# Drawing up the engines' order with the timeline simulator in a hybrid attention and long-convolution block

## The chip, the cores and the metric

The kernel runs on one core of one Trainium2 chip. Five engines with an instruction queue each do the work: TensorE (matmuls; "PE" in the profile, its weight loads "PEld"), VectorE ("DVE"), ScalarE ("ACT"), GpSimd ("POOL") and SyncE ("SP"), which here only issues DMAs. Each engine takes its own instructions strictly in the order in which the program lists them; between engines, semaphores tell when an input is there or a buffer is free. The metric is the time of one execution in microseconds, as the median of three runs.

## The reference

One trunk layer of a diffusion backbone over 1024 latent tokens of width 1024, with 256 context tokens beside them, all in float32:

```python
h = modulate(rmsnorm(x, norm1_g[i]), sh1, sc1)
q, k, v, hv, hx1, hx2, gna, ghy = jnp.split(h @ w_in[i], IN_SPLITS, axis=-1)
y_na = neighbourhood_attention(to_heads(q), to_heads(k), to_heads(v),
                               to_heads(k_c), to_heads(v_c), na_rpb[i])
y_hy = hyena_mixer(hv, hx1, hx2, *hy_params)
x = x + g1 * gated_merge(gna, ghy, y_na, y_hy, w_na_o[i], w_hy_o[i], w_out[i])
h2 = modulate(rmsnorm(x, norm2_g[i]), sh2, sc2)
x = x + g2 * swiglu(h2, ffn_w1[i], ffn_w3[i], ffn_w2[i])
...
return rmsnorm(x, final_g)
```

The shifts, scales and gates (sh1, sc1, g1 and so on) are rows of silu(c) @ w_ada + b_ada. The attention has 8 heads of width 64; each query sees a window of 8 x 16 of the 16 x 64 grid, with a learned bias, and all context keys. The Hyena mixer is a short convolution followed by two gated long convolutions over all 1024 tokens, with filters that a small network makes, computed by Fourier transforms. The feed-forward part has a hidden width of 2816.

## The kernel before

**Arithmetic.** Most products run on operands that are split into a high and a low part of a faster float32 form: `split` (L175 casts on ScalarE, L176 subtracts on VectorE), and `gemm` or `product` then does three matmuls for each 128-deep step, low by high, high by low, high by high. Transposes and Fourier matrices use plain float32. The feed-forward products use a scheme with seven block products in place of eight (operands named h2_1 to h2_7).

**Stages.** `hidden` loads x, makes the first norm's transposed activations and the first adaptive-norm rows from eight 1 MB pieces of w_ada (tiles `wada`, L297, three buffers; products at L299 into `ada_ps`). `project` makes the 40 column blocks of the input projection, each in two halves of 512 tokens, 24 matmuls a half (L195, `in_ps`). Beside it, `side` runs the Hyena filters (`filters`: `filt_ps` L363, times the decay factors `dec` on VectorE at L370), the remaining adaptive-norm rows (`ada_rows`, VectorE at L890 on tiles `wal`), and then four long convolutions (`conv`, transforms `dft_ps` L442 to L444, with matrices `matf` and `mati`). Each convolution goes through seven steps, in which the forward transform of a class, the product with the filter's spectrum, the inverse transform and the combination on VectorE are a step apart from each other. Then `attention` takes 32 items (a pair of heads, a row block, a column block): scores (`s_ps`, L766 and L769), softmax (VectorE L774, ScalarE L775), transposes (`pt_ps` L786), copy (`pts`, L790), values (L800), copy to `yrow` (L807); the last projection halves and the Hyena output (`hy_ps`) run between the items. `mix` and `rows` merge both branches (`na_ps`, `out_ps` L1109), then `ffn_early`, `ffn_up` (`x_ps`, `y_ps`, `z_ps`, L1171) and `ffn_down` (`dx_ps`, `dy_ps`, `dz_ps`, L1340) follow, with `close` and `finish` for the output.

**What sets the order.** The kernel's Python code traces all instructions in one program order; generators are merged by weights (`_merged`, with `SIDE` = 496 for the side work against 39 for the projection, and yields that tell the weight of a step). The order on each engine is not that one. When the TileContext closes, a scheduler draws it up: it steps a simulated machine through time, and whenever an engine of that machine can take another instruction, it gives it the ready one of the lowest priority number, which is the place in the program order. Ready means that, on the simulated machine, what it depends on is done and a buffer of its pool is free. So the durations that the simulated machine assigns decide which of two instructions gets ahead of the other, on the five engines and among the DMAs of each queue, and which buffer of a ring a tile gets. On the chip the lists are then fixed: nothing is picked again.

Two devices bend this. `tc.high_priority()` gives what is traced in it an earlier priority (projection weights, the short convolution's taps, some loads of the feed-forward part). `tc.keep_in_program_order(x)` ties an instruction behind the one traced before it on its engine, whatever the simulated machine says. So pinned are the filters' matmuls but the first of each four, the score, transpose and value matmuls of attention, the projection's matmuls after `self.pinned` is set (the part that runs between attention items), the Hyena output's matmuls, the first matmul of each early feed-forward product, and loads of w2 in `ffn_down`. The matmuls of the projection before that, the transforms, the merge and the rest of the feed-forward part are free.

The library has two simulated machines. The plain one, used before, gives each instruction a duration and an engine; the timeline simulator turns each into a list of events on devices (an engine's sequencer, its queue of issued instructions, the engine itself, the DMA hardware) and steps these. The first is also the one whose optimism about landed inputs the library's text on `keep_in_program_order` speaks of.

Of the kernel before, what the change touches and what calls it, by code (L numbers as in the profile page):

```python
# [1455 lines left out]
def program(nc, shapes):  # L1456
    args = {n: nc.dram_tensor(f"in_{n}", s, F32, kind="ExternalInput").ap() for n, s in shapes.items()}
    out = nc.dram_tensor("out_y", (T, D), F32, kind="ExternalOutput").ap()
    with tile.TileContext(nc) as tc:
        Block(tc, args, out).run()  # L1460


# [9 lines left out]
```

## Time and profile before

| | |
|---|---|
| median of 3 runs (lowest, highest) | 1711.23 us (1708.59, 1711.89) |
| profiled execution, span from first to last instruction | 1711.4 us |
| that span against the median | 0.2 us above it |
| TensorE busy | 1657.6 us, 97% |
| its weight loads | 1307.2 us, 76% |
| VectorE, ScalarE, GpSimd busy | 1230.1, 662.6, 153.3 us |
| mean granted TensorE clock | 0.993 |
| moved by DMA | 282.48 MB, 165 GB/s |

The profile shows one execution. A line of a timeline gives start, busy time, engine, source line, operation and tiles; a bracket at its end tells how long the engine was idle before it and what ended that. "PEclk" is the granted share of TensorE's full clock. Lines of waits give the waiting engine and tile, what it waited for, the total, how often, and the longest.

### The profile page before, as it was taken

The page shows a single profiled execution, that of the slowest core. Times are in us where ns is not written, and L with a number is a line of the kernel's source. Part 1 is how long each engine was busy: PE and PEld are TensorE (multiplying, and loading weights), DVE is VectorE, ACT ScalarE, POOL GpSimd, SP SyncE. Part 2 cuts the span into 40 slices and gives each one's busy share as a digit, 9 for nine tenths or more (in the row PEclk, how much of TensorE's full clock was granted, in tenths as well). Part 3 has the DMA queues.
Part 4 walks back from the last instruction along what each step waited for, and adds up shares of the span by engine and source line. Part 5 has one row for each costly group of instructions (what it writes and reads, how often), then busy time and mean ns, then how long its engine had stood idle before and what let it go on. Part 6 is the DMA issues. An engine that isn't in the chain of part 4 may idle for free.

```text
span 1711.4 us, 22611 instructions
## 1 busy us (share of the span) xinstructions
PE 1657.6 (97%) x8124; PEld 1307.2 (76%) x8124; DVE 1230.1 (72%) x2076; ACT 662.6 (39%) x1141; POOL 153.3 (9%) x274
## 2 busy tenths in 40 slices
PE   6898999999999999999999999999999999999997
PEld 2676776777777778888787888888888888878886
DVE  3697586699995966465865967867865566479576
ACT  4621221312221224455654315733333333355455
POOL 0100211101010014020200000010101011000000
PEclk9999999999999999999999999999999999999999
DMA  9276854645553456344657524333423223395334
GB/s 364 103 255 199 266 173 158 215 139 187 167 201 137 160 187 186 126 148 131 197 174 245 187 65 160 124 124 117 160 99 110 94 99 109 105 383 177 98 120 154
DMA packets 114517, 282.48 MB, mean 165 GB/s; under 512 B 15840, under 2 KB 24676, under 8 KB 112102
## 3 DMA queue, kind: packets, MB, share of 16 engines
q1 hardware_dynamic: 94472, 219.99, 38.6%
q0 software_dynamic: 19280, 60.60, 10.5%
q8 instruction: 64, 1.05, 0.3%
q10 hardware_dynamic: 653, 0.44, 0.1%
q14 instruction: 48, 0.39, 0.1%
HBM read 213.60 MB, written 67.39 MB: 164 GB/s over the span
## 4 chain that ended last, share of the span: by engine, by line
PE 65%; issue 10%; DVE 4%; DMA 2%; ACT 1%; POOL 1%; SPq 0%; DVEq 0%; POOLq 0%; ACTq 0%
PE x_ps L1171 15%; PE in_ps L195 12%; PE z_ps L1171 7%; PE dx_ps L1340 6%; PE out_ps L1109 4%; PE dz_ps L1340 3%; PE hy_ps L195 2%; PE y_ps L1171 2%; PE dft_ps L442 2%; PE pt_ps L800 2%; PE pt_ps L786 2%; PE na_ps L195 2%; PE dy_ps L1340 1%; PE s_ps L766 1%; PE dft_ps L444 1%
## 5 line engine op out<-in xcount | busy, mean ns | idle before, releaser
L195 PE MATMUL in_ps<-hTh,wl 128*128 128x512 f32 x640 | 260.0, 407 | 0.9 <-ACT proj L614 0.5
L195 PE MATMUL in_ps<-hTl,wh 128*128 128x512 f32 x640 | 254.5, 398 | 0.4 <-DVE hTl L176 0.2
L195 PE MATMUL in_ps<-hTh,wh 128*128 128x512 f32 x640 | 253.9, 397 | 0.0
L195 PEld LDWEIGHTS in_ps<-hTh,wl 128*128 128x128 f32 x640 | 121.5, 190 | 32.2 <-issue 5.6
L195 PEld LDWEIGHTS in_ps<-hTl,wh 128*128 128x128 f32 x640 | 121.8, 190 | 27.1 <-DVE hTl L176 1.8
L195 PEld LDWEIGHTS in_ps<-hTh,wh 128*128 128x128 f32 x640 | 121.6, 190 | 26.9 <-issue 0.4
L175 ACT CAST wh<-wr 128x1024 fp32r<-128x1024 f32 (+1 forms) x56 | 51.9, 926 | 141.4 <-PE in_ps L195 110.0
L176 DVE TENSOR_TENSOR wl<-wr,wh 128x1024 fp32r<-128x1024 f32 (+1 forms) x56 | 59.8, 1067 | 63.2 <-ACT wh L175 63.1
L176 DVE TENSOR_TENSOR ol<-ws,oh 128x512 fp32r<-128x512 f32 x88 | 60.4, 688 | 50.6 <-ACT oh L175 50.3
L176 DVE TENSOR_TENSOR ol<-ar,oh 128x512 fp32r<-128x512 f32 x77 | 52.8, 687 | 47.7 <-ACT oh L175 47.7
L175 ACT CAST oh<-ar 128x512 fp32r<-128x512 f32 x77 | 47.9, 622 | 84.4 <-PE dx_ps L1340 33.1
L175 ACT CAST oh<-ws 128x512 fp32r<-128x512 f32 x88 | 54.7, 622 | 57.1 <-PE x_ps L1171 27.5
L442 PE MATMUL dft_ps<-a,matf 128*128 128x512 f32 x128 | 67.1, 606 | 5.0 <-DVE a L430 4.1
L775 ACT ACTIVATE pe<-pe,mx 128x640 f32<-128x640 f32 x64 | 52.6, 822 | 48.9 <-DVE mx L774 48.9
L1340 PE MATMUL dx_ps<-ol,oh 128*128 128x512 f32 x176 | 68.7, 390 | 1.7 <-DVE ol L176 1.7
L774 DVE CUSTOM_DVE_ANT_0 pe<-s_ps,bias 128x640 f32<-128x640 f32 x64 | 50.1, 820 | 28.1 <-PE s_ps L769 28.1
L1340 PE MATMUL dx_ps<-oh,ol 128*128 128x512 f32 x176 | 67.4, 390 | 1.9 <-DVE ol L176 1.9
L1340 PE MATMUL dx_ps<-oh 128*128 128x512 f32 x176 | 68.5, 389 | 0.0
L176 DVE TENSOR_TENSOR ol<-wr,oh 128x512 fp32r<-128x512 f32 x70 | 48.0, 688 | 22.3 <-ACT oh L175 22.2
L175 ACT CAST oh<-wr 128x512 fp32r<-128x512 f32 x70 | 43.3, 622 | 52.3 <-PE x_ps L1171 16.0
L890 DVE SCALAR_TENSOR_TENSOR aacc<-wal,cs,aacc 128x512 f32<-128x512 f32 x56 | 41.8, 747 | 23.1 <-DMA wal<-in_w_ada 22.5
L1111 DVE TENSOR_TENSOR x<-x,out_ps 128x512 f32<-128x512 f32 x64 | 42.6, 683 | 15.2 <-PE out_ps L1109 15.0
(394 smaller groups left out, 4193.7 us busy)
## 6 DMA issues: line engine op xcount, KB each, us to landing
wr<-in_w SPq DMA_DIRECT2D x52, 512.0 KB, 3.4
wr<-in_w_in SPq DMA_DIRECT2D x40, 512.0 KB, 4.2
ar<-g SPq DMA_DIRECT2D x77, 256.0 KB, 2.8
wal<-in_w_ada SPq DMA_DIRECT2D x64, 256.0 KB, 4.1
matf<-in_dft_f SPq DMA_DIRECT2D x32, 384.0 KB, 4.7
bias<-in_rpb SPq DMA_DIRECT2D x64, 192.0 KB, 3.7
g<-t POOLq DMA_DIRECT2D x47, 256.0 KB, 3.0
w<-in_w SPq DMA_DIRECT2D x44, 256.0 KB, 5.4
```

The costliest lines, as they stand in the source:

```text
L175: self.nc.scalar.copy(hi, src)
L176: self.nc.vector.tensor_sub(lo, src, hi.bitcast(F32))
L195: mm = nc.tensor.matmul(ps, ww[:, k * P:(k + 1) * P], xx[:, k, pos:pos + width], start=(i == 0), stop=(i == n - 1))
L442: nc.tensor.matmul(ps, m[:, 0], v.rearrange("p a b -> p (a b)"), start=True, stop=False)
L774: nc.vector.tensor_tensor_reduce(pe, ps[:, 256:896], bt, -1.0, 3e38, ALU.add, ALU.min, mx[:, 0:1])
L775: nc.scalar.activation(pe, pe, AF.Exp, bias=mx[:, 0:1], scale=-1.0, accum_out=mx[:, 1:2])
L786: pin(nc.tensor.transpose(pt[:, at:at + P], pe[:, c * P:(c + 1) * P], self.ident))
L890: nc.vector.scalar_tensor_tensor(acc, w, c, acc, op0=ALU.mult, op1=ALU.add)
L1109: nc.tensor.matmul(ps, gg[x][:, tk], ww[y][:, sl], start=(i == 0), stop=(i == n - 1))
L1111: nc.vector.tensor_add(x1[:, sl], x1[:, sl], ps)
L1171: mm = nc.tensor.matmul(ps, w[u][:, k * P:(k + 1) * P], x[v][:, k, :], start=(start and k == 0 and i == 0), stop=(stop and k == 3 and i == 2),
L1340: nc.tensor.matmul(ps[j], x[u][:, j * P:(j + 1) * P], w[v], start=(start and i == 0 and c == 0), stop=(stop and i == N - 1 and k == len(re ...
```

## The change

The scheduler steps the timeline simulator in place of the plain machine. No instruction is added, removed or altered, no tile, pool, pin or weight. What may come out otherwise is the order on each engine and DMA queue, the buffer that a tile gets, and with these the semaphore waits.

```diff
@@ -1456,7 +1456,7 @@
 def program(nc, shapes):
     args = {n: nc.dram_tensor(f"in_{n}", s, F32, kind="ExternalInput").ap() for n, s in shapes.items()}
     out = nc.dram_tensor("out_y", (T, D), F32, kind="ExternalOutput").ap()
-    with tile.TileContext(nc) as tc:
+    with tile.TileContext(nc, schedule_with_timeline_sim=True) as tc:
         Block(tc, args, out).run()
```

## The prediction

> **What bounds the kernel now.** I read the page first: which engine is busy, and for how much of the span.
>
> ```profile
> span 1711.4 us, 22611 instructions
> PE 1657.6 (97%) x8124; PEld 1307.2 (76%) x8124; DVE 1230.1 (72%) x2076; ACT 662.6 (39%) x1141; POOL 153.3 (9%) x274
> GB/s 364 103 255 199 266 173 158 215 139 187 167 201 137 160 187 186 126 148 131 197 174 245 187 65 160 124 124 117 160 99 110 94 99 109 105 383 177 98 120 154
> ```
>
> TensorE works 97% of the span; it is without work for 1711.4 - 1657.6 = 53.8 us. The profiled span lies 0.2 us above the median of the three runs, 1711.23 us, so a sum made against it holds for the median too. The change leaves every instruction as it is and alters only in which order each engine takes its own. It can then gain at most where TensorE waits, and it can lose wherever TensorE is now kept fed. So the second view is the busy time by stage: start (to 75 us), filters beside the input projection (to 350), long convolutions beside it (to 560), the way over to attention (to 680), attention (to 925), merge (to 1070), the up half of the feed-forward part (to 1490) and its down half.
>
> ```profile
> core 0: us, PE busy (x) PEld busy (x) DVE busy (x) ACT busy (x) POOL busy (x), PEclk, DMA share, GB/s
> 0.00:75.00 75.00, 57.54 (x276) 33.19 (x276) 41.73 (x72) 46.06 (x75) 2.48 (x9) 1.00 0.59 230
> 75.00:350.00 275.00, 258.52 (x1188) 193.29 (x1187) 201.75 (x292) 61.62 (x98) 36.02 (x61) 0.96 0.64 209
> 350.00:560.00 210.00, 210.00 (x887) 159.91 (x885) 183.43 (x317) 48.79 (x69) 15.84 (x23) 1.00 0.52 172
> 560.00:680.00 120.00, 118.13 (x524) 92.19 (x524) 93.43 (x166) 34.91 (x55) 24.78 (x45) 1.00 0.55 180
> 680.00:925.00 245.00, 240.50 (x1848) 194.50 (x1847) 153.11 (x352) 132.52 (x248) 28.38 (x51) 1.00 0.51 157
> 925.00:1070.00 145.00, 143.85 (x646) 117.89 (x644) 111.86 (x164) 55.48 (x88) 4.26 (x8) 1.00 0.47 158
> 1070.00:1490.00 420.00, 419.06 (x1848) 344.36 (x1848) 282.39 (x442) 170.99 (x294) 39.18 (x73) 1.00 0.33 112
> 1490.00:1711.40 221.40, 210.01 (x920) 171.83 (x918) 162.44 (x276) 112.17 (x214) 2.40 (x5) 0.99 0.56 188
> sum 1711.40, PE 1657.63 PEld 1307.17 DVE 1230.14 ACT 662.56 POOL 153.34; mean PE 207.20 PEld 163.40 DVE 153.77 ACT 82.82 POOL 19.17
> ```
>
> Taking busy from length, the idle time is 17.5, 16.5, 0, 1.9, 4.5, 1.2, 0.9 and 11.4 us. The reader is to see how lopsided this is: from 350 to 1490 us, two thirds of the kernel, only 8.5 us can be won, and every microsecond of a new misfit is lost. The filter stage, with 16.5 us, is the one place where another order has something to find. There the clock column also stands at 0.96.
>
> [...]
>
> **The filter stage, where a gain can be.** TensorE takes its instructions in the drawn order, so one matmul drawn too early holds up all behind it. Two such places, from the timelines:
>
> ```profile
> 83.45 0.39 PE L195 MATMUL in_ps<-hTh,wh 128*128 128x512 f32 x1
> 86.26 1.13 PE L363 MATMUL filt_ps<-fw,hid 64*128 64x256 f32 x6 [2.42 <-DVE fv L370]
> ...
> 87.90 0.63 PE L195 MATMUL in_ps<-hTl,wh 128*128 128x512 f32 x1
> ...
> 90.46 0.54 PE L195 MATMUL in_ps<-hTl,wh 128*128 128x512 f32 x1
> ```
>
> ```profile
> 137.25 0.39 PE L195 MATMUL in_ps<-hTh,wh 128*128 128x512 f32 x1
> 137.25 0.19 PEld L195 LDWEIGHTS in_ps<-hTh,wl 128*128 128x128 f32 x1
> 137.48 0.39 PE L195 MATMUL in_ps<-hTh,wl 128*128 128x512 f32 x1
> 141.46 1.39 DVE L370 TENSOR_TENSOR fv<-filt_ps,dec 128x512 f32<-128x512 f32 x2 [3.67 <-DMA dec<-in_decay]
> ...
> 142.21 2.07 PE L363 MATMUL filt_ps<-fw,hid 64*128 64x256 f32 x6 [4.33 <-DVE fv L370]
> ...
> 144.80 0.63 PE L195 MATMUL in_ps<-hTh,wh 128*128 128x512 f32 x1
> ...
> 148.64 0.47 PE L195 MATMUL in_ps<-hTh,wh 128*128 128x512 f32 x1
> ```
>
> At 137.48 a half of the projection (24 matmuls for 512 tokens) has begun, is cut by six filter matmuls, and goes on at 144 us: its other matmuls had all they need. The filter matmuls wait for a PSUM bank that VectorE frees, and VectorE waits 3.67 us for the decay factors' DMA. The plain model had those landed sooner. A model that follows the transfers more closely would draw the filter matmuls later, behind ready ones. Each stall has a second price: after it the projection's matmuls start 0.43 us apart (nine of them in 148.64 - 144.80 = 3.84 us) instead of 0.23 (137.25 to 137.48): 3.84 - 9 x 0.228 = 1.79 us. After the first stall six take 90.46 - 87.90 = 2.56 us, 1.19 us too much. So the two are worth 4.33 + 1.79 and 2.42 + 1.19: **-9.7 us**, which I take in full. Bounds: 0, if the new order misses as often elsewhere, and all 16.5 us of the stage with 1.79 + 1.19 on top.
>
> [...]
>
> **The start.** The adaptive-norm rows need eight 1 MB loads, and the order on SP's queue decides what goes before them.
>
> ```profile
> L299 PE MATMUL ada_ps<-wada,cs 128*32 128x512 f32 x64 | 13.7, 959 | 6.3 <-DMA wada<-in_w_ada 6.3
> ```
>
> A simulator in which the first product ends later frees the three wada buffers later, and puts other ready loads ahead on the queue. One 512 KB load at the first slice's 364 GB/s takes 0.524 / 0.364 = 1.4 us. I take one such load: **+1.4 us**; bounds are the 6.3 us gained and, with four of the x loads in front, 5.8 lost.
>
> **Attention, where a loss can be.** Here all TensorE instructions of scores, transposes, values and the projection or Hyena matmuls between them are held in program order (keep_in_program_order), so the new model can't move TensorE at all; it can only move ScalarE, VectorE and the DMA issues under it. With no other matmul to step in, a ScalarE copy that comes late is paid directly. Two such places now:
>
> ```profile
> 821.39 1.32 PE L786 MATMUL pt_ps<-ident,pe 128*128 128x128 f32 x10 [1.15 <-ACT yrow L807]
> ...
> 922.71 0.66 PE L800 MATMUL pt_ps<-pts,vc 128*64 128x128 f32 x8 [1.55 <-ACT yrow L807]
> ```
>
> One costs (1.15 + 1.55) / 2 = 1.35 us. ScalarE is busy 132.5 of 245 us, 54%. If its order is redrawn, an item's copy finds something in its way in 0.54 x 32 items = 17 cases: 17 x 1.35 = 23.4 us, less the 4.5 us that the stage idles already: **+18.9 us**. What queues behind the late copy is the item's value matmuls, then the projection's or Hyena's 12 or 24 matmuls, then the next scores. The lower end is -4.5 (every wait of today gone); the upper is all 32 items at 1.55, 49.6 - 4.5 = +45.1. I take the middle term since it goes by how often the engine is occupied; it is the least certain number here.
>
> **The up half.** It idles 0.9 us in 420.
>
> ```profile
> L176 DVE TENSOR_TENSOR ol<-ws,oh 128x512 fp32r<-128x512 f32 x88 | 60.4, 688 | 50.6 <-ACT oh L175 50.3
> ...
> L175 ACT CAST oh<-ws 128x512 fp32r<-128x512 f32 x88 | 54.7, 622 | 57.1 <-PE x_ps L1171 27.5 <-PE z_ps L1171 13.0 <-issue 8.3
> ```
>
> ```profile
> 1115.44 2.72 PE x_ps L1171 x12
> ```
>
> An operand costs a cast and a subtraction, 0.62 + 0.69 = 1.31 us, and its product 2.72 us. Seven operand pairs (five in one ring, two in the other) let six be ready ahead: 6 x 2.72 = 16.3 us of cover. So I cost the stage at **0**. If the cover went once in each of the 22 weight tiles' turns it would be 22 x 1.31 = +28.8; nothing can be gained. The convolutions up to 560 us also stand at 0: TensorE is full, and a late side is covered as the third rival says. Merge and down half hold 1.2 and 11.4 us of idle time, the last mostly the closing chain after the last matmul, which no order shortens; I take 0, with 3 us either way inside the range.
>
> **Sum.** 1711.4 - 9.7 + 1.4 + 18.9 = **1722.0 us**, 0.6% slower.
>
> **The rivals.**
>
> First, faster. Two further stalls of the filter stage would go as well:
>
> ```profile
> 233.55 1.54 PE L442 MATMUL dft_ps<-a,matf 128*128 128x512 f32 x2 [1.93 <-DVE a L430]
> ...
> 265.27 2.07 PE L363 MATMUL filt_ps<-fw,hid 64*128 64x256 f32 x6 [3.48 <-DVE fv L370]
> ...
> 267.87 0.63 PE L195 MATMUL in_ps<-hTl,wh 128*128 128x512 f32 x1
> ...
> 271.70 0.39 PE L195 MATMUL in_ps<-hTl,wh 128*128 128x512 f32 x1
> ```
>
> They add 1.93 and 3.48 + (271.70 - 267.87 - 9 x 0.228 = 1.78): with the 9.7 it is -16.9 us, 1694.5. It needs attention to stay as it is. For it speaks that most waits of this stage end on a DMA or on VectorE that waited for one (the row below), which is just what a plainer model misjudges. With all idle time of the stage, 16.5 us, the slow pace after three stalls, 4.8, and attention's 4.5 gone it would be 1685.6.
>
> ```profile
> DVE fv L370 <- DMA dec<-in_decay: 20.3, 14, 3.7
> ```
>
> Second, no change: the pins fix TensorE's order in attention and in the Hyena output, and data dependences fix much of the rest, so that the gain of the filter stage meets an equal loss: 1711. Against it speaks that TensorE's order in the filter stage isn't pinned as a whole, so a net within 3 us needs luck. That the option would do nothing at all belongs here too.
>
> Third, much slower: the side work becomes the bound. Filters and convolutions hand work to TensorE and back. If the new model commits TensorE to matmuls further ahead of time, a transform that becomes ready finds a whole half of a projection before it:
>
> ```profile
> matf<-in_dft_f SPq DMA_DIRECT2D x32, 384.0 KB, 4.7
> ...
> mati<-in_dft_i SPq DMA_DIRECT2D x16, 384.0 KB, 3.1
> ```
>
> ```profile
> 636.66 29.58 PE in_ps L195 x129
> ...
> 694.31 5.67 PE in_ps L195 x24
> ```
>
> The convolutions make 16 forward rounds (32 matrices, half of them for the filters) and 16 inverse ones, 32 hops; a half in the way is 5.67 us. TensorE isn't idle meanwhile: it does projection work that it would do later. The reserve for this is the unpinned run at 636.66, 29.58 us. So it decides from the sixth late hop on (5 x 5.67 = 28.4). One hop in three late: 11 x 5.67 - 29.6 = +32.8, 1744; every second: 16 x 5.67 - 29.6 = +61.1, 1772. For it speaks that VectorE is busy 183.4 of 210 us there and has little to catch up with; against it that the side's steps are written one stage ahead of each other, which hides a hop shorter than a stage.
>
> **How the numbers follow.** What a measurement of this kernel can tell from no change is about 0.2%, 3.4 us. Chances: forecast (attention loses more than the filter stage gains) 0.33; side bound 0.19; faster 0.36; no change 0.12. So slower 0.52, same 0.12, faster 0.36. The forecast's own range is 1715 to 1735: one projection stall less or more and attention at half or at one and a half. The range for 8 in 10 reaches to 1686, the end of the faster case, and to 1772, the side late at every second hop.
>
> **What would show it.** Filter stage: TensorE busy above 258.5 of 275 us, no bracket over 2 us before filt_ps, clock column at 1.00. Attention: busy share falling below 240.5 of 245 with ScalarE's yrow or pts copies named as releasers. Side bound: the run of 129 gone, and waits of dft_ps or of VectorE on dft_ps beyond 560 us. Wrong altogether would be a loss of more than 5 us in the up half, which I cost at 0, or an attention stage shorter than today's while the total is slower.

## The result, and the profile after

The changed kernel takes 1762.85 us (median of four runs, 1762.10 to 1766.62) where the kernel before, run beside it, takes 1710.82 (1708.59 to 1711.89): a ratio of 1.0316, 95% interval 1.0296 to 1.0335. It is 52.0 us slower. The profiled execution took 1763.08 us with a span of 1761.3, so it stands for the median.

First the page of the changed kernel: span and busy time of each engine.

```profile
span 1761.3 us, 22558 instructions
PE 1671.2 (95%) x8124; PEld 1319.8 (75%) x8124; DVE 1227.1 (70%) x2076; ACT 655.6 (37%) x1141; POOL 152.9 (9%) x274
```

The same 8124 matmuls run. TensorE's idle time went from 53.8 to 1761.3 - 1671.2 = 90.1 us, +36.3; its busy time went from 1657.6 to 1671.2, +13.6, with the mean granted clock at 0.974 instead of 0.993. So a good quarter of the 49.9 us by which the span grew is not idle time but the same matmuls run more slowly, at the lower granted clock.

Then the busy time by stage of the changed kernel, the windows cut where the same stages lie in it.

```profile
core 0: us, PE busy (x) PEld busy (x) DVE busy (x) ACT busy (x) POOL busy (x), PEclk, DMA share, GB/s
0.00:85.00 85.00, 61.77 (x290) 38.04 (x291) 42.31 (x72) 45.66 (x75) 4.54 (x15) 0.84 0.52 208
85.00:390.00 305.00, 282.25 (x1288) 212.72 (x1289) 215.26 (x318) 68.13 (x108) 36.31 (x61) 0.96 0.60 197
390.00:587.00 197.00, 193.43 (x800) 145.96 (x798) 166.81 (x289) 41.01 (x59) 12.80 (x19) 1.00 0.50 168
587.00:710.00 123.00, 105.46 (x428) 81.05 (x428) 88.33 (x152) 27.57 (x45) 24.25 (x44) 0.93 0.49 161
710.00:973.00 263.00, 254.94 (x1909) 206.12 (x1909) 161.03 (x369) 138.31 (x260) 29.16 (x52) 0.98 0.49 153
973.00:1119.00 146.00, 144.77 (x653) 119.14 (x654) 111.93 (x165) 55.81 (x90) 4.26 (x8) 1.00 0.44 157
1119.00:1538.00 419.00, 418.32 (x1842) 343.54 (x1842) 280.34 (x442) 167.67 (x294) 38.91 (x72) 1.00 0.32 112
1538.00:1761.30 223.30, 210.23 (x920) 173.22 (x918) 161.05 (x274) 111.44 (x214) 2.70 (x5) 0.98 0.55 186
```

Idle time by stage is 23.2, 22.8, 3.6, 17.5, 8.1, 1.2, 0.7 and 13.1 us, where the kernel before had 17.5, 16.5, 0, 1.9, 4.5, 1.2, 0.9 and 11.4. The way over to attention, nearly full before, now idles 17.5 of 123 us, for its length more than any other stage but the start; the start, the filters and attention each lose some too. The up half is as dense as it was.

Idle time alone doesn't tell where the end moved, since work can change places between stages. So I also compare when the same matmul starts in both traces (first or last start of a tile's matmuls, us from the span's start). Beside them stand four of the experiments that follow.

| matmul | before | after | e2_hand | t_pe4 | t_pe4all | b_dma30 |
|---|---|---|---|---|---|---|
| first in_ps | 37.4 | 47.6 | 46.6 | 46.8 | 38.8 | 37.5 |
| first dft_ps of the filters | 112.3 | 131.3 | 130.6 | 132.5 | 124.6 | 120.9 |
| first dft_ps on mati (inverse) | 349.3 | 389.2 | 388.2 | 348.8 | 352.7 | 342.9 |
| first yh_ps | 556.5 | 587.0 | 586.0 | 560.9 | 558.2 | 533.3 |
| last dft_ps | 620.1 | 648.1 | 646.9 | 621.2 | 620.4 | 594.0 |
| first s_ps | 666.2 | 708.6 | 697.1 | 679.2 | 666.4 | 640.1 |
| s_ps of the 21st item | 840.4 | 888.9 | 875.0 | 859.7 | 843.4 | 811.1 |
| last hT_ps | 1082.5 | 1129.6 | 1116.0 | 1100.4 | 1086.3 | 1053.5 |
| end of the span | 1711.4 | 1761.3 | 1749.4 | 1730.8 | 1715.0 | 1682.4 |

After minus before is +10.2 at the first projection, +30.5 at the first yh_ps, +42.4 at the first score, +48.6 at the 21st item, +47.1 at the last transposes of the merge and +49.9 at the end. The kernel loses about 10 us in the start, 20 beside filters and convolutions, 12 on the way to attention, 6 at one place in attention, and 1 in everything after.

Up to the last dft_ps both kernels run the same number of matmuls, and so they do from there to the first score. The rows of these two stretches, in the same columns as above, of the kernel before:

```profile
0.00:620.06 620.06, 584.80 (x2583) 430.04 (x2584) 473.62 (x761) 168.24 (x259) 57.00 (x98) 0.98 0.56 190
620.06:666.18 46.12, 46.12 (x212) 37.64 (x211) 38.24 (x64) 15.15 (x25) 20.30 (x37) 1.00 0.83 270
```

and of the changed kernel:

```profile
0.00:648.07 648.07, 591.87 (x2583) 436.88 (x2584) 473.10 (x761) 166.38 (x259) 56.32 (x98) 0.95 0.54 182
648.07:708.62 60.55, 49.90 (x212) 39.97 (x210) 39.41 (x67) 14.70 (x25) 21.59 (x39) 0.92 0.66 214
```

In the first stretch TensorE is idle for 56.2 us instead of 35.3, in the second for 10.7 instead of 0; the rest of the 42.4 us is busy time at a lower clock, 0.95 and 0.92 where it was 0.98 and 1.00. By the last transform no more projection work has been done than before, and just as much is left for the way to the first score.

The filter stage. VectorE's waits between 110 and 350 us (waiting tile, what for, total, times, longest), of the kernel before:

```profile
DVE aacc L890 <- DMA wal<-in_w_ada: 20.8, 13, 4.9
DVE fv L370 <- DMA dec<-in_decay: 14.4, 10, 3.7
...
DVE a L430 <- PE dft_ps L444: 3.1, 4, 1.1
DVE fv L370 <- PE filt_ps L363: 1.1, 1, 1.1
```

and of the changed kernel:

```profile
DVE a L430 <- PE dft_ps L444: 26.5, 14, 4.0
DVE fv L370 <- DMA dec<-in_decay: 20.9, 10, 7.1
DVE fv L370 <- PE filt_ps L363: 7.7, 1, 7.7
...
DVE aacc L890 <- DMA wal<-in_w_ada: 5.1, 5, 2.1
```

Two things have got worse. VectorE waits longer for the decay factors, so this planner doesn't draw their use later as I had thought. And it waits for TensorE's filter and transform products, 34.2 us together where it was 4.2: I read this as the filter chain standing behind other matmuls in TensorE's order; t_pe4 below tests it. One thing has got better: the wait for the rows of w_ada (wal) fell by 15.7 us, so that all of VectorE's waits in this window together only rose from 61.5 to 69.9. TensorE pays later: the taps of the short convolution (L600), which free its banks, are drawn behind filter work: from 232.8 us on VectorE works without a pause, and the taps that TensorE waits for run from 246.1. In TensorE's timeline of the changed kernel, with the idle time in front in brackets:

```profile
251.31 0.79 PE L195 MATMUL in_ps<-hTh,wl 128*128 128x512 f32 x1 [5.09 <-DVE proj L600]
```

The way over to attention. ScalarE's timeline of the changed kernel:

```profile
689.16 0.62 ACT L175 CAST krh<-kraw 128x512 fp32r<-128x512 f32 x1 [6.06 <-DVE kraw L697]
689.68 1.04 ACT L175 CAST wh<-wr 128x1024 fp32r<-128x1024 f32 x1
694.53 0.62 ACT L175 CAST krh<-kraw 128x512 fp32r<-128x512 f32 x1 [3.81 <-DVE kraw L697]
695.05 1.08 ACT L614 ACTIVATE proj<-in_ps 128x512 f32<-128x512 f32 x2
```

and TensorE's at the same time:

```profile
695.70 0.79 PE L195 MATMUL in_ps<-hTh,wl 128*128 128x512 f32 x1 [7.63 <-ACT proj L614]
```

TensorE has no free bank for the next projection half. The evictions that would free two of them (L614) stand on ScalarE's queue behind casts of rotated keys, and those wait for VectorE, which waits for loads (3.43 and 2.13 us for kraw, up to 685.87 and 691.25). In the order before, no more than three casts follow each other there without an eviction; here six stand in front of two evictions. The unpinned run of 129 projection matmuls that covered this stretch before is divided otherwise: behind the last dft_ps stand runs of 79, 14 and 99 where there were 49, 14 and 129, 192 in both. The stalls lie within the run of 99, from 671 us on.

Attention loses at one place, on VectorE, in the changed kernel:

```profile
860.71 1.29 DVE L176 TENSOR_TENSOR yal<-yrow,yah 128x512 fp32r<-128x512 f32 x2
...
862.54 0.68 DVE L176 TENSOR_TENSOR wl<-wr,wh 128x512 fp32r<-128x512 f32 x1
863.13 0.69 DVE L176 TENSOR_TENSOR krl<-kraw,krh 128x512 fp32r<-128x512 f32 x1
...
865.66 0.55 DVE L779 TENSOR_SCALAR pe<-pe,mx 128x640 f32<-128x640 f32 x1
```

```profile
866.35 1.30 PE L786 MATMUL pt_ps<-ident,pe 128*128 128x128 f32 x5 [4.36 <-DVE pe L779]
```

The softmax's last step (L779) finds splits and preparing steps drawn in front of it, and the pinned transposes wait 4.36 us.

### The profile page after: what moved, and what is told of

Same layout as the page of the kernel before. It is cut to its first block, busy times and chain, and to the rows that moved or that the text cites. A ratio compares the mean times of both kernels' runs of the same rounds, so it can differ in the third digit from the quotient of the medians.

```text
span 1761.3 us, 22558 instructions
## 1 busy us (share of the span) xinstructions
PE 1671.2 (95%) x8124; PEld 1319.8 (75%) x8124; DVE 1227.1 (70%) x2076; ACT 655.6 (37%) x1141; POOL 152.9 (9%) x274
## 4 chain that ended last, share of the span: by engine, by line
PE 53%; issue 3%; DMA 2%; DVE 2%; ACT 1%; POOL 0%; SPq 0%; DVEq 0%; POOLq 0%; ACTq 0%
PE x_ps L1171 14%; PE z_ps L1171 6%; PE dx_ps L1340 6%; PE in_ps L195 5%; PE out_ps L1109 4%; PE dz_ps L1340 3%; PE hy_ps L195 3%; PE pt_ps L800 2%; PE pt_ps L786 2%; PE y_ps L1171 2%; PE na_ps L195 2%; PE dy_ps L1340 2%; PE s_ps L766 1%; DMA yhraw<-yh 1%; PE s_ps L769 1%
## 5 line engine op out<-in xcount | busy, mean ns | idle before, releaser
L195 PE MATMUL in_ps<-hTh,wl 128*128 128x512 f32 x640 | 262.6, 411 | 27.4 <-ACT proj L614 15.1
L195 PE MATMUL in_ps<-hTh,wh 128*128 128x512 f32 x640 | 258.6, 404 | 0.0
L195 PE MATMUL in_ps<-hTl,wh 128*128 128x512 f32 x640 | 258.4, 404 | 0.0
L175 ACT CAST oh<-ar 128x512 fp32r<-128x512 f32 x77 | 48.0, 623 | 89.8 <-PE dx_ps L1340 36.3
L1340 PE MATMUL dx_ps<-oh,ol 128*128 128x512 f32 x176 | 58.0, 391 | 3.7 <-DVE ol L176 3.7
L430 DVE SCALAR_TENSOR_TENSOR a<-x,b 128x512 f32<-128x512 f32 x64 | 42.0, 684 | 26.5 <-PE dft_ps L444 26.5
L1111 DVE TENSOR_TENSOR x<-x,out_ps 128x512 f32<-128x512 f32 x64 | 42.4, 682 | 13.8 <-PE out_ps L1109 13.8
L176 DVE TENSOR_TENSOR ol<-wr,oh 128x512 fp32r<-128x512 f32 x70 | 47.6, 686 | 6.1 <-ACT oh L175 6.0
```

The costliest lines, as they stand in the source:

```text
L175: self.nc.scalar.copy(hi, src)
L176: self.nc.vector.tensor_sub(lo, src, hi.bitcast(F32))
L195: mm = nc.tensor.matmul(ps, ww[:, k * P:(k + 1) * P], xx[:, k, pos:pos + width], start=(i == 0), stop=(i == n - 1))
L430: nc.vector.scalar_tensor_tensor(av, x, -g if j else g, b[:, 0], op0=ALU.mult, op1=ALU.add)
L1111: nc.vector.tensor_add(x1[:, sl], x1[:, sl], ps)
L1340: nc.tensor.matmul(ps[j], x[u][:, j * P:(j + 1) * P], w[v], start=(start and i == 0 and c == 0), stop=(stop and i == N - 1 and k == len(re ...
```

## The experiments

All of them change only what the planner is told or what it must keep in order; the computation is that of both kernels. Names with b_ start from the kernel before (plain planner), all others but n1 from the changed one. Each ran beside the kernel before, whose medians were 1709.1 to 1710.6.

**Is 1711 one lucky drawing?** A greedy order can change in many places for a small cause, so first a control with the plain planner.

```diff
 def program(nc, shapes):
-    args = ...
+    from concourse.hw_specs import TRN2Spec as S; setattr(S, 'PE_CYCLE', S.PE_CYCLE * 1.01); args = ...
```

> The plain planner of before, with the TensorE cycle in its table 1 per cent longer and nothing else changed: a control for how far the time moves when the order is merely drawn a little otherwise. Theory, the plain planner's order is good by its model, not by luck: the median stays within 4 of 1710.8. Rival, 1710.8 is one lucky draw for which the kernel's constants were set, and any redrawing costs: 1720 or more.

Measured: 1710.70 us, ratio 1.0008 (0.9996 to 1.0021), though the order differs in some 520 places, counted place by place on the five engines. So a small redrawing by itself costs nothing that can be measured. The change itself moves some 5700 places, and no control here is that large.

**The start.**

```diff
-            nc.sync.dma_start(w, a["w_ada"][k, :, 0:2048])
+            pin(nc.sync.dma_start(w, a["w_ada"][k, :, 0:2048]))
...
-        self.ready[4] = self.weights(wpool, a["w_in"][4])
+        self.ready[4] = self.weights(wpool, a["w_in"][4], pin=pin)
```

(pin is keep_in_program_order; the loads of x and ctx and the other weight tile likewise.)

> Timeline planner kept; only SyncE's loads of the start (wada, x, ctx, the first two weight tiles) are held in the order in which the program writes them, which is the order that the plain planner had drawn. Theory, the start's loss comes from SyncE's order there and is carried to the end: the first projection matmul, at 47.55 us in the changed kernel and at 37.38 before, comes back to 37 to 39 us, and the median falls by 8 to 10 from 1762.9, to 1753 to 1755. Rival, the ten microseconds are absorbed by later waits for VectorE in the filter stage, which would come earlier or be longer: the first projection matmul is early but the median stays at 1760 or more. Everything behind the start is drawn anew by the planner, so a few us either way can come from that; the landmarks tell where.

Measured: the first in_ps at 39.4 us, as the theory had it, and a median of 1760.51, as the rival had it. The eight microseconds shrink to 3.3 by the first dft_ps of the filters, which now starts at 128.0 instead of 131.3. The start was lost on SyncE's order, but nearly all of it is lost to the filter chain anyway.

**The way over to attention.**

```diff
-        self.nc.scalar.copy(hi, src)
+        self.held(self.nc.scalar.copy(hi, src))
...
-                nc.scalar.activation(st[:, sl], pt, AF.Copy if f < 32 else AF.Sigmoid)
+                self.held(nc.scalar.activation(st[:, sl], pt, AF.Copy if f < 32 else AF.Sigmoid))
...
         for n in range(6):
-            next(prepared)
+            next(prepared); (yield) if n in (1, 4) else None
...
-                next(attention)
-                for _ in range(AHEAD):
-                    next(proj)
+                self.held = tc.keep_in_program_order
+                for i in range(AHEAD):
+                    next(attention if i < 3 else iter([0])); next(proj)
```

> Timeline planner kept; the six preparing steps of attention are written between the last unpinned projection halves instead of ahead of them, and ScalarE's casts and projection evictions are held in that order until the first attention item. Theory, the handover's loss is ScalarE's evictions (line 614) standing behind casts krh and qrh that wait for VectorE and for loads: the stretch from the last dft_ps matmul to the first s_ps matmul, 60.5 us in the changed kernel and 46.1 before, falls to 46 to 50, and the median by 10 to 14, to 1749 to 1753. Rival, the order of ScalarE only shows a lateness of VectorE or of the loads: the stretch stays over 56 and the median within 4 of 1762.9.

Measured: 1750.93 us, ratio 1.025 (1.0229 to 1.0272), 11.9 less than the changed kernel. The stretch from the last dft_ps (646.9) to the first s_ps (697.1) is 50.2 us in place of 60.5, and 46.1 before. TensorE's waits from 585 to 712 us, first of the changed kernel, then of this one:

```profile
PE in_ps L195 <- ACT proj L614: 15.1, 4, 7.6
```

```profile
PE in_ps L195 <- ACT proj L614: 6.2, 2, 3.9
```

So most of what this stretch had lost, 10.3 of 14.4 us, goes by the order of ScalarE's casts and evictions, and of the preparing steps of attention that the edit places with them.

**The filter stage, from TensorE's and from the loads' side.** Two ways in which the late taps could come about:

```diff
-                nc.tensor.transpose(ps[:, j * P:(j + 1) * P], ...)
+                (self.tc.keep_in_program_order if j == 0 and not self.fine else id)(nc.tensor.transpose(ps[:, j * P:(j + 1) * P], ...))
...
-            for t in turn:
-                self.tokens(psc, *t)
+            for n, t in enumerate(turn):
+                self.tokens(psc, *t, at=0 if self.fine or n else 1)
...
-                if group is groups[0]:
-                    next(between)
+                (not self.fine and not h and turn) and self.tokens(psc, *turn[0], to=1); group is groups[0] and next(between)
```

> Timeline planner kept; the token transposes (tm_ps) of a projected feature are no longer drawn together behind both halves of the next one: the first group of four is written and held behind its first half, the second behind its second half. Theory, TensorE's loss between 200 and 460 us comes from its own order, which puts these transposes back to back although each needs the buffer that the one before it frees: the waits of tm_ps for line 571 over 0.8 us, 10.4 us together in the changed kernel, go, and the median falls by 8 to 12, to 1751 to 1755. Rival, VectorE is late there (it waits 7.1 us for a dec load at 218 us), so the wait only moves to in_ps behind line 600, now 13.1 us together: the median stays over 1758.

Measured: 1759.78 us. The waits stay and only change places: 1.2, 5.2 and 0.7 us of tm_ps near 240 us, and 2.9, 4.9 and 5.1 of in_ps behind line 600, which end at 247, 310 and 368. The rival holds.

```diff
-                        w = pool.tile([P, 512], F32, tag="wal2", name="wal", bufs=4)
+                        w = pool.tile([P, 512], F32, tag="wal2", name="wal", bufs=2)
```

> Timeline planner kept; the rows of w_ada that ada_rows reads have two buffers instead of four, so that fewer of these 256 KB loads can stand ahead of the filters' dec loads. Theory, the eight wal loads issued between 209 and 217 us make the dec load of 218.2 land at 225.7, VectorE waits 7.1 us for it and is late with the taps of line 600 afterwards: VectorE's wait for dec falls under 3 us, in_ps waits under 4 us for line 600 in place of 5.4 and 5.2, and the median falls by 6 to 12, to 1751 to 1757. Rival, the taps are late because of TensorE's and VectorE's own order: the median stays over 1758.

Measured: 1769.44 us, slower still. Over the span VectorE's wait for dec falls from 25.7 to 19.0 us, but its wait for the wal loads, which now come singly, rises from 9.5 to 33.7. The theory missed its own mark (19.0 us, no fall of the median). The run doesn't settle what the burst of wal loads costs, since it puts 24.2 us of new waits for wal in the place of 6.7 for dec.

**The place in attention.**

```diff
-                nc.vector.reciprocal(mx[:, 2:3], mx[:, 1:2])
-                nc.vector.tensor_scalar_mul(pe, pe, mx[:, 2:3])
+                self.drawn(nc.vector.reciprocal(mx[:, 2:3], mx[:, 1:2]))
+                self.drawn(nc.vector.tensor_scalar_mul(pe, pe, mx[:, 2:3]))
...
-                for _ in attention:
-                    next(hyena, None)
+                self.drawn = tc.keep_in_program_order
+                for n, _ in enumerate(attention):
+                    next(hyena, None); self.drawn = self.drawn if n < 3 else lambda i: i
```

(The preparing steps, splits and ghy products are held likewise.)

> Timeline planner kept; from the first attention item without a projection half on, for four items, VectorE's softmax, preparing steps, ya splits and ghy products are held in the order in which the program writes them, so that lines 778 and 779 of an item stand ahead of the ya splits. Theory, the 6.1 us that the changed kernel loses between attention items 16 and 20 are VectorE's order: the difference to before does not grow there, from +42.4 to less than +44 in place of +48.6, and the time falls by 4 to 6, to 1757 to 1759. Rival, the work is simply too much for VectorE at this place in any order: the stall of pt_ps behind pe moves to the next item and the time stays over 1761.

Measured: 1768.93 us, two runs. The softmax is no longer late, but the Hyena output's weights, split on the same engine, are. TensorE's timeline of this kernel:

```profile
861.47 0.76 PE L195 MATMUL hy_ps<-yhh,wl 128*128 128x512 f32 x1 [6.68 <-DVE wl L176]
```

A second such stall, of 4.54 us, follows at 894.83. Neither order is good. The kernel before has no wait over 1.2 us at this place, so "too much for VectorE in any order" is wrong as well: in its trace the two kinds of work alternate finely. That VectorE's order is the cause is read from the traces; no run here takes this loss away from the timeline planner.

**The price of a transfer.** My prediction had the timeline planner correct the plain one's optimism about loads. The same correction can be made in the plain planner's table, in both directions:

```diff
 def program(nc, shapes):
-    args = ...
+    from concourse.hw_specs import TRN2Spec as S; setattr(S, 'DMA_START_FIXED_NS', S.DMA_START_FIXED_NS + 1500); args = ...
```

> The plain planner of before, whose fixed time of a transfer's start is raised from 1300 to 2800 ns and nothing else: the correction that the prediction had expected of the changed planner. Theory, two filter-stage stalls of before (2.1 us of dft_ps at 231.3 and 3.7 us of filt_ps at 261.4) come from the plain planner's belief that loads land early: they go, the order elsewhere is hardly touched, and the median falls by 3 to 8, to 1703 to 1708. Rival, what is drawn later for it is lost as reserve elsewhere: 1712 or more.

> Plain planner, fixed time of a transfer's start 4300 ns in place of 1300 (2800 gave 1686.8). Theory, the loads of the filter stage took 2.7 to 7.5 us from issue to landing, so a price nearer to that still gains or holds: VectorE's wait for dec 12 us or less and the median 1680 to 1690. Rival, what is drawn later for it costs elsewhere, so that 2800 was near the best: 1695 or more.

> Plain planner, fixed time of a transfer's start 300 ns in place of 1300, the other way round. Theory, the time follows the planner's belief about loads: VectorE's wait for dec rises over 23 us and the median to 1720 or more. Rival, the gain at 2800 ns was one good drawing and no effect of the price: the median is within 6 of 1710.4 either way.

(+ 3000 in b_dma30 and - 1000 in b_short.) Measured, for 300, 1300, 2800 and 4300 ns: 1740.91, 1709.1 to 1710.4, 1686.81 and 1684.77 us. The ratios to before are 1.0171 (1.0142 to 1.0199), 1, 0.9868 (0.9842 to 0.9894) and 0.9844 (0.9822 to 0.9867). That is far more than the 3 to 8 us that I expected. VectorE's wait for dec over the whole span is 17.8, 20.3, 11.4 and 12.5 us, so at 300 ns it doesn't rise as I had said, and at 4300 it misses its mark of 12 narrowly. The loss at 300 ns lies elsewhere, about half of it before the inverse transforms, whose first is 14.8 us later than before. For 4300 ns, TensorE's and VectorE's busy time over the span of 1682.4 us, and the row from 200 to 450 us:

```profile
PE 1646.5 (98%) x8124; PEld 1303.1 (77%) x8124; DVE 1229.6 (73%) x2076; ACT 661.6 (39%) x1141; POOL 153.4 (9%) x274
```

```profile
200.00:450.00 250.00, 250.00 (x1101) 188.96 (x1100) 211.04 (x349) 64.45 (x96) 28.27 (x40) 1.00 0.56 181
```

The same row of the kernel before, and then of the changed kernel:

```profile
200.00:450.00 250.00, 243.66 (x1066) 182.28 (x1065) 205.55 (x334) 60.88 (x91) 25.17 (x36) 0.98 0.56 179
200.00:450.00 250.00, 227.02 (x972) 167.93 (x970) 179.89 (x286) 60.18 (x91) 30.08 (x47) 0.95 0.53 175
```

With dearer transfers TensorE has no gap there any more, where it idled 6.3 us, and VectorE does 211 us of work instead of 206. The changed kernel lies on the other side, with 23.0 us idle and 180 us of VectorE's work. How long such loads take from issue to landing, from the kernel before (size, median us):

```profile
wal<-in_w_ada SPq DMA_DIRECT2D x64, 256.0 KB, 4.1
dec<-in_decay SPq DMA_DIRECT2D x32, 256.0 KB, 3.2
```

By the trace these loads of 256 KB take 4.1 and 3.2 us. What sets that time, no run here shows.

Now the same correction in the timeline planner's table:

```diff
+    from concourse.hw_specs import TRN2Spec as S; setattr(S, 'DGE_DMA_DELAY', {k: v + 1500 for k, v in S.DGE_DMA_DELAY.items()}); args = ...
```

> Timeline planner, in whose table every queue's delay before a transfer starts is 1500 ns longer: the same correction that took the plain planner from 1710.4 to 1686.8. Theory A, the timeline planner loses by the same belief that loads land early, VectorE being drawn to wait for dec (25.7 us in the filter stage, 20.3 before, 11.4 with the corrected plain planner) and ScalarE for the rotated keys: VectorE's wait for dec falls under 16 us, the stretch from the last dft_ps to the first s_ps under 54 us, and the median to 1735 or less. Rival B, the loss comes from the other things that this planner steps through, above all its queues: the waits only move, and the median stays between 1745 and 1770.

Measured: 1755.76 us, ratio 1.0248 (1.0213 to 1.0282). Rival B holds: 7.1 us are gained, with runs between 1749.7 and 1760.2; VectorE's wait for dec is still 20.0 us, and its wait for dft_ps is 30.8. What costs this planner its 52 us is not, in the main, this price of a load.

**The planner's queues.** The timeline simulator models that an engine's queue takes instructions ahead of the engine: 35 for TensorE and 12 for the others, in its table. An instruction is chosen when it enters the queue.

```diff
+    from concourse.hw_specs import TRN2Spec as S; setattr(S, 'ENG_ISSUE_QUEUE_DEPTH', {k: 1 for k in S.ENG_ISSUE_QUEUE_DEPTH}); args = ...
```

> Timeline planner kept, but in its table of how many instructions an engine's queue takes ahead (35 for TensorE, 12 for the others) every entry is 1, so that it chooses an instruction only when the engine is nearly free. Theory, the loss comes from choosing far ahead, so that an eviction or a tap that becomes ready meanwhile finds longer work already drawn before it: the waits of in_ps for line 600 and line 614 shrink and the median falls to 1735 or below. Rival, the loss comes from this model's durations, or from any order other than the one that the constants were set for: the median stays between 1750 and 1775.

Measured: 1959.94 us. The loss lies all over the kernel: even from the last hT_ps to the first dx_ps, the up half, it takes 438 us instead of 407. With every queue at 1 the planner draws a far worse order. I haven't followed which of the five queues does that.

```diff
+    from concourse.hw_specs import TRN2Spec as S; S.ENG_ISSUE_QUEUE_DEPTH = dict.fromkeys(S.ENG_ISSUE_QUEUE_DEPTH, 100); args = ...
```

> Timeline planner whose table of queue depths has 100 for every engine in place of 35 for TensorE and 12 for the others (with 1 everywhere it took 1959.9). Theory, full queues hold the planner's own engines back, so that work which VectorE could do in the filter stage is drawn late: VectorE's busy time between 200 and 450 us rises from 180 to over 195 (206 before), and the median falls to 1745 or less. Rival, 12 and 35 are already deep enough and the loss is elsewhere: VectorE stays under 190 there and the median between 1752 and 1775.

> Timeline planner with queue depths of 100 and the delay before a transfer 2200 ns on every queue (650 and 784 in the changed kernel). Theory, depth and transfer price are the two causes and add: 1735 or less, with VectorE's wait for dec under 18 us. Rival, as for the deeper queues alone, or the gain of 7 us of the transfer price by itself: 1748 or more.

Measured: 1842.22 and, with the longer transfer delay as well (2200 on every queue), 1832.56 us. Deeper is worse too, so the theory as I wrote it is wrong in sign. VectorE's waits from 110 to 350 us in t_q4 hint at what deepens: 25.9 us for TensorE's transforms and 16.3 for its filter products, 42.2 together after 34.2 with 35 and 12 entries; the longest single wait went from 7.7 to 9.7. That is only 8.0 us of a far larger loss, but it points to TensorE's queue: products of the filter chain, ready now, may stand behind projection matmuls chosen earlier. So I changed TensorE's alone, and VectorE's and ScalarE's alone:

```diff
+    from concourse.hw_specs import TRN2Spec as S; S.ENG_ISSUE_QUEUE_DEPTH = {**S.ENG_ISSUE_QUEUE_DEPTH, mybir.EngineType.PE: 4}; args = ...
```

> Timeline planner whose table lets TensorE's queue take 4 instructions ahead in place of 35; the other engines keep 12. Theory, the filter chain is late because each of its hops finds up to 35 projection matmuls (35 x 0.22 = 7.7 us) chosen ahead of it: the first dft_ps comes 8 us or more earlier than 131.3, VectorE's wait for filt_ps falls from 7.7 to under 3 us and its busy time between 200 and 450 us rises from 180 to over 195, and the median falls to 1740 or less. Rival, TensorE's depth only matters as cover, and with less of it TensorE waits more often: the median is 1763 or more, as with depth 1 everywhere.

```diff
+    ... S.ENG_ISSUE_QUEUE_DEPTH = {**S.ENG_ISSUE_QUEUE_DEPTH, mybir.EngineType.DVE: 4, mybir.EngineType.Activation: 4}; args = ...
```

> Timeline planner whose table lets VectorE's and ScalarE's queues take 4 instructions ahead in place of 12; TensorE keeps 35. Theory of the run above: little changes, 1755 to 1770. Rival, it is VectorE's own choosing ahead that puts long filter operations before taps (line 600): the waits of in_ps for line 600 fall from 13.1 to under 5 us and the median to 1750 or less.

Measured: 1732.80 us with TensorE's queue at 4 (ratio 1.0131, 1.0112 to 1.0150), 30.1 less than the changed kernel; 1760.97 with the other two. VectorE's waits of t_pe4 from 110 to 350 us, and its row from 200 to 450:

```profile
DVE fv L370 <- DMA dec<-in_decay: 12.1, 8, 4.0
DVE a L430 <- PE dft_ps L444: 10.5, 13, 1.4
...
DVE fv L370 <- PE filt_ps L363: 7.1, 2, 5.4
```

```profile
200.00:450.00 250.00, 239.32 (x1049) 179.37 (x1048) 207.26 (x340) 60.76 (x92) 29.54 (x45) 0.98 0.56 185
```

VectorE waits 17.6 us for TensorE's products instead of 34.2, and 12.1 for dec instead of 20.9; it is busy 207 us instead of 180. The first inverse transform starts at 348.8 us after the same 1459 matmuls as before (349.3); the changed kernel had run 1575 by then. That TensorE's entry in the planner's table costs about 30 us is shown, and 26.1 of them stand at the first yh_ps. How it does so is less sure, for two of my marks missed: the first dft_ps isn't earlier (132.5 us), and the wait for filt_ps hardly shrinks. The gain comes behind the first dft_ps, and the largest fall among VectorE's waits is that for the transforms (L430), from 26.5 to 10.5.

**Together.**

```diff
+    from concourse.hw_specs import TRN2Spec as S; S.DGE_DMA_DELAY = dict.fromkeys(S.DGE_DMA_DELAY, 2200); args = ...
```

on top of e1_start's and e2_hand's edits (t_handdma), and with TensorE's queue at 4 as well (t_pe4all):

> Timeline planner with SyncE's start loads and ScalarE's handover held as in e1_start and e2_hand, and the delay before a transfer 2200 ns on every queue. Theory, the causes add (2.4 and 11.9 and 7.1 us by their own medians): 1739 to 1745, the first s_ps not over 25 us later than before. Rival, they overlap at the handover, where the corrected price and the held order remove the same waits: 1746 to 1752.

> Timeline planner with TensorE's queue at 4, SyncE's start loads and ScalarE's handover held, and the delay before a transfer 2200 ns on every queue (without the shorter queue 1743.0). Theory, TensorE's choosing ahead is the cause that was left: 1700 to 1725. Rival, it is not: 1740 or more.

Measured: 1742.97 us (ratio 1.0194, 1.0173 to 1.0215) and 1713.92 us (1.0022, 1.0009 to 1.0035). Start, handover and transfer price take away 19.9 us, near the 21.4 of their single gains; TensorE's queue takes 29.1 more, near the 30.1 that it gave alone. With these four the timeline planner is 3.6 us behind the plain one. The first score starts at 666.4 us, 0.3 after that of before; the 21st item is 3.0 late, so most of what is left arises at the place in attention. This brings the time back, but it doesn't name every cause: the dearer transfer helps the plain planner too, by 23.6 us at 2800 ns, and against that version (1686.81) the best timeline order is still 27.1 us behind. What those 27 us are stays open.

The version that beats both kernels is the plain planner with the dearer transfers, 1684.77 us.

## Why the prediction was right or wrong

The direction held, and so did the range for 8 in 10; the forecast's own range, 1715 to 1735, did not, and the size was too small by 41 us. That the direction came out was luck: it hung on the attention term of +18.9, without which the sum is a gain, and that term measured +6.1 on another engine. The steps that failed are the gain in the filter stage, taken in full, and the way over to attention, which had no term.

**The filter stage, -9.7.** Wrong in sign: from the first in_ps to the first yh_ps the changed kernel loses 20.3 us, past the bound of 0 that I had set. One half of the step came true. "A model that follows the transfers more closely would draw the filter matmuls later, behind ready ones": the filters' first transform has 240 projection matmuls in front of it instead of 182, and TensorE's waits before the filter matmuls shrink, as its waits between 30 and 600 us show, first before and then after.

```profile
PE filt_ps L363 <- DVE fv L370: 10.7, 4, 4.3
```

```profile
PE in_ps L195 <- DVE proj L600: 12.2, 4, 5.1
PE tm_ps L569 <- ACT tm L571: 9.7, 8, 2.5
...
PE filt_ps L363 <- DVE fv L370: 3.4, 2, 2.9
```

What failed is "which I take in full": it set at nothing what products drawn later do to VectorE. As I read the traces, VectorE gets them late, and its taps and ScalarE's copies follow late; TensorE now waits 12.2 us for taps and 9.7 for copies where it had waited under 0.5 for either. Nor were the loads foreseen better: VectorE's wait for dec rose from 20.3 to 25.7 us over the span. The remark that the plain planner's stalls come from loads believed to land early fits b_dma and b_dma30, and was worth more than I priced: with dearer transfers its span gets 27 to 29 us shorter. What was wrong is the belief that this change makes that correction.

**The start, +1.4.** Mis-sized, and past the bound of 5.8: the first projection matmul is 10.2 us late. I counted one x load more in front on SyncE's queue. Eight x loads and a weight tile now stand ahead of the fourth piece of w_ada, where there were two x loads, and TensorE's own order put transposes of x between the products, which wait for VectorE. TensorE's timeline of the changed kernel:

```profile
15.22 1.06 PE L299 MATMUL ada_ps<-wada,cs 128*32 128x512 f32 x8 [1.44 <-DMA wada<-in_w_ada]
23.56 0.66 PE L248 MATMUL hT_ps<-ident,x 128*128 128x128 f32 x2 [7.28 <-DVE x L289]
```

It matters little: e1_start gave back 8.1 us at this point and 2.3 at the end.

**Attention, +18.9 on ScalarE.** Mis-sized and on the wrong engine: +6.1 us, at one place, on VectorE. The step "an item's copy finds something in its way in 0.54 x 32 items" takes the share of time that an engine is busy for the chance that a planner puts work in front of a copy (and 17 x 1.35 is 23.0; the 23.4 needs 17.3 cases). The planner didn't: from the first item to the seventeenth the two kernels keep the same distance, 42.4 us.

**The way over to attention, not in the sum.** +11.9 us from the first yh_ps to the first score. I costed the convolutions at 0 and had no row for what follows them: "TensorE is full, and a late side is covered as the third rival says". The 192 projection matmuls behind the last dft_ps are all still there, but in the new order ScalarE frees their banks late: from 585 to 712 us TensorE waits 15.1 us for evictions (L614), where it waited 0.5 before and waits 6.2 in e2_hand.

**The up half, 0, and merge and down half, 0.** Right: +0.8 us between the last transposes of the merge (+47.1) and the first dx_ps (+47.9), about -1.5 in the merge, +2.0 in the down half.

**The rivals.** The third, the side as the bound, comes nearest: its sentence "If the new model commits TensorE to matmuls further ahead of time" names the cause that t_pe4 showed. I gave it 0.19 because "the side's steps are written one stage ahead of each other, which hides a hop shorter than a stage". The trace refutes that: 14 waits of VectorE for a transform, up to 4.0 us each, where there had been 4 of up to 1.1. That 1763 lies between its 1744 and 1772 is luck, though, for its sum works otherwise. It says that "TensorE isn't idle meanwhile" and that late hops cost time once the reserve behind the transforms is used up. Here the reserve is untouched, and up to the first score TensorE idles 31.6 us more and is busy 10.8 us longer with the same matmuls. A hop is held for 1.9 us on average (26.5 / 14), not by a whole projection half of 5.67. Of the marks that I had set for it, the run of 129 is gone, though not its matmuls; of the waits for dft_ps most come before 350 us, and only one of 3.2 us lies beyond 560.

The first rival, faster, failed with the filter stage. The second, no change, failed too. How deep the chip's own queues are, no run here shows. Of deeper tables in the planner only 100 on every engine was run (t_q4, 1842.22 us), and it did worse than 35 and 12.

## What to carry to other kernels

A simulator that models more devices isn't for that a better planner (1762.85 us here, 1710.82 with the plain one): a greedy choice made at the entry of a modelled queue is made early, and, as I read these traces, short steps of a chain between two engines then queue behind bulk work (VectorE's waits for TensorE's filter and transform products fell from 34.2 to 17.6 us with TensorE's entry at 4). Stalls that such an order takes away are no gain before you have asked where the delayed work is waited for next. If a profile shows an engine waiting for loads that the planner took for landed, correct the price of the load in the planner, try both directions, and run a tiny change as a control, since even that moves hundreds of instructions. And sum up by stages with a row for every handover between them: that a handover costs nothing today hangs on other engines' order too, so it is a term with a price, not a zero.

## What the runs showed that I had not expected

TensorE's busy time changes with the order by far more than the 1.79 and 1.19 us that the prediction read at two stalls of the filter stage. The same 8124 matmuls kept TensorE busy for 1646.5 us in b_dma30, 1657.6 before and 1671.2 in the changed kernel, where the granted clock averaged 0.994, 0.993 and 0.974. Between the first and the last lie 24.7 us of busy time, which no count of instructions or of idle gaps shows, and the mean clock only in part: between b_dma30 and the kernel before it differs by 0.001 and the busy time by 11.1 us. From the kernel before to the changed one, 36.3 us more of idle time came with 13.6 us more of busy time. A slow pace after stalls is part of it: in the changed kernel the eight projection matmuls from 696.29 us on, behind the wait of 7.63, start 0.43 us apart, those from 699.58 on 0.23. How much of the whole it makes up, no run here shows.
